# Staging weights in 1024-column buffers instead of 512-column ones in a one-core hybrid decoder step

## The chip, the core and the metric

The kernel runs on one NeuronCore of a Trainium2 chip as a single launch. The metric is the device time of one execution in microseconds. TensorE (PE in the profile, its weight loads PEld), VectorE (DVE), ScalarE (ACT), GpSimd (POOL) and SyncE (SP) each run their own instruction list in order and wait for each other through semaphores. SP starts the plain DMAs and POOL the indirect ones. The 16 DMA engines carry both.

## The reference

One layer of a decoder for 1024 prompt tokens and 32 sampled tokens, model width 1024, all in float32:

```
proj = x @ w_in                                # 1024 -> 9744 columns
o_a  = three dilated sliding-window softmax attentions, mixed by their log-sum-exp
o_b  = gated linear attention in chunks of 64, normalised, times silu(rb)
x    = layer_norm(a*x + (sigmoid(ga)*(o_a@w_branch_a) + sigmoid(gb)*(o_b@w_branch_b)) @ w_out)
q    = normalised (x @ w_peer_query)           # 8 heads
expert, gate = top 16 of 128 x 128 product keys per head     # 128 experts per token
act  = gelu(x . u_table[expert])
x    = layer_norm(a*x + sum(gate * act * v_table[expert]))
```

The caches of keys and values, moved on by the new tokens, and the states of the linear attention are outputs too.

## The kernel before

A float32 product is made of three TensorE passes (`mm3`, lines 184 to 187): every operand is split into a high part and a rest, both stored as fp32r, and high x high, rest x high and high x rest are added up. The split of a weight tile is two instructions: ACT copies the staged tile into the high part (`copy_act`, line 143) and DVE subtracts it to get the rest (line 158). Weights come through `load_w_` (line 170): one DMA of 128 x 512 floats into a staging buffer `wst` (three of them), a high part `wh` (four) and a rest `wl` (four). A staging buffer is free again when DVE has subtracted; a `wh` when TensorE has used it.

The program has these stretches. Prompt half b=0 (512 tokens) with the 32 sampled tokens, and then b=1 (512 tokens): projections (`dense_T` with 4 of 8 row blocks for one load, `rows_of` with one row block for one load), attention, linear attention, output projection, PEER queries and top-k. Then the PEER mixer, in two ways at once:

- `peer_gather` (line 1216), for half of the prompt tokens and the sampled ones: for each of 128 experts of a token tile, POOL gathers 128 rows of `u` (line 1233) or `v` (line 1254) into one of four `gr` buffers, and DVE makes one pass of 128 x 1024 over it (lines 1239 and 1272). That makes 1088 gathers, of which the last 32 of one tile are summed on TensorE.
- `peer_dense` (line 1330), for the other 512 tokens: all 16384 experts in 128 steps `e` of 128 experts. `hidden(e)` loads 128 columns of `uT` (two loads of 512) and makes 24 matmuls; `gelu` puts the result aside, seven steps ahead of its use. `values(e)` loads and splits 128 rows of `pv` (two loads of 512). `weights(e)` multiplies the gelu by the gate matrix `G` (line 1364), which is loaded for 8 steps at a time with two DMAs of 1 MB (line 1383, tensor `Gd`), and splits the product into two `tq` tiles. `out` makes 24 matmuls for each `e`. Eight steps are 384 matmuls of 512 columns; below they are called a block.

The ten `pg` pages hold the inputs of `hidden` (four), `G` and the split `v`. The order on each engine is not the order of the code: a scheduler places every instruction by priority and by its own estimate of time, and buffers that come free bound it. Gathers have the lowest priority and fill gaps. Weight loads get a higher priority than their place in the code. Buffers are named in rows by the helper's tag (`wst`, `wh`, `wl`, `pg`, `tq`, `gr`). The memory that the DMAs of POOL need for their descriptors lies in the same on-chip memory as the buffers, and its size is set where the program object is made, in `kernel` (line 1693).

Of the kernel before, what the change touches and what calls it, by code (L numbers as in the profile page):

```python
# [21 lines left out]
P = 128  # L22
# [59 lines left out]
def tile_hybrid_step(ctx, tc, I, O, dbg=None):  # L82
# [31 lines left out]
    def sb(shape, tag, bufs, dt=F32):  # L114
        return sp.tile(list(shape), dt, tag=tag, bufs=bufs, name=nm(tag))
# [42 lines left out]
        V.tensor_sub(lo, src, hi)  # L158

    copies = []  # L160
    due, hush = [0.0], [False]

    def load_w(src, shape):
        keep = tc.cur_priority
# [3 lines left out]
        return r  # L168

    def load_w_(src, shape):  # L170
        st = sb(shape, "wst", 3)
        ld = nc.sync.dma_start(st, src)
        due[0] += CRATE
        for _ in range(2):
            if copies and not hush[0] and due[0] >= 1:
                due[0] -= 1
                with tc.issue_after(ld.ins):
                    nc.sync.dma_start(*copies.pop(0))
        hi = sb(shape, "wh", 4, F32R)
        lo = sb(shape, "wl", 4, F32R)  # L180
        split_into(st, hi, lo)
        return hi, lo

    def mm3(out, lh, ll, rh, rl, first, last):
# [312 lines left out]
    def rows_of(toks, src, xs, cols=None, stag=0):  # L497

        outs = [(ps() if i < 4 else (pb if busy[0] else pc)())[:m] for i, m in toks]
        def products(p_, i, m, k, w):  # L500
            if i < 4 and cols:
                h, l = [cols(v, i) for v in xs(k, 0, T)]
            else:
                h, l = xs(k, i * P, i * P + m)
            mm3(p_, h, l, *w, k == 0, k == 7)


        for k in range(8):
            tick()
            if k <= 8 - stag:  # L510
                ws = []
            ws.append(load_w(src[:, k], [P, 512]))
            if k < 8 - stag:
                for p_, (i, m) in zip(outs, toks):
                    products(p_, i, m, k, ws[0])
        for p_, (i, m) in zip(outs, toks):
            for j in range(stag):
                products(p_, i, m, 8 - stag + j, ws[j])
        return outs


    def phase_a(b):

        mark(f"att{b}")
        dec = b == 0
        busy[0] = b == 1
        shapes = lambda d: (TW if d else T, [(0, 256), (256, TW)] if d else [(0, 512)], [(i, P) for i in range(4)] + [(4, NS)] * d)
        W, segs, toks = shapes(dec)
        row0 = lambda i: 2 * T if i == 4 else b * T + i * P
# [11 lines left out]
        def dense_T(src, nk, xs, width=P):  # L541

            out = [(ps(), c0, c1) for (c0, c1) in (segs0 if xs is x else segs)]
            for k0 in range(0, nk, 4):
                wh, wl = load_w(src[:, k0:k0 + 4], [P, 4, width])
                for k in range(k0, k0 + 4):
                    for (p_, c0, c1) in out:
                        h, l = xs(k, c0, c1)
                        mm3(p_[:width, :c1 - c0], wh[:, k - k0], wl[:, k - k0], h, l, k == 0, k == nk - 1)
            return out  # L550

        def proj_T(ci):
# [777 lines left out]
    def peer_dense(x1T, toks):  # L1330
# [4 lines left out]

        def hidden(e):
            p_ = ps()
            for k0 in (0, 4):
                wh, wl = load_w(I["uT"][e][:, k0:k0 + 4], [P, 4, P])
                for k in range(4):  # L1340
                    h, l = x1T(k0 + k, 0, T)
                    mm3(p_, wh[:, k], wl[:, k], h, l, k0 + k == 0, k0 + k == 7)
            return p_

        def values(e):
            v = page([P, 2, D], F32R)
            for hf in range(2):
                st = sb([P, 512], "wst", 3)
                c = slice(hf * 512, (hf + 1) * 512)
                nc.sync.dma_start(st, vrows[e][:, c])  # L1350
                split_into(st, v[:, 0, c], v[:, 1, c])
            return v

        def gelu(e):
# [351 lines left out]
```

## Time and profile before

| | |
|---|---|
| device time, median of 3 runs | 4181.1 us (4180.77 to 4182.56) |
| the profiled execution | 4168.93 us, of which the span of its instructions is 4167.2 us |
| PE busy | 3739.9 us (90%), 18338 matmuls |
| DVE busy | 3147.9 us (76%), 7279 instructions |
| ACT busy | 1444.7 us (35%), 2958 instructions |
| POOL busy | 1345.5 us (32%) |
| DMA | 1118.18 MB, mean 268 GB/s |
| PEER mixer's dense loop | first multiplication by G at 2598.6 us of the span, last block of G asked for at 4046.0 us |

Busy shares are means over stretches that differ, so the page's 40 slices and a table of stretches are read before any sum. A matmul of 512 columns is shown with some 0.4 us, but the next one starts 0.23 us later, since they overlap; what a stretch holds is read from counts of matmuls in a time. An idle stretch of an in-order engine is put down to the instruction that ended it.

### The profile page before, as it was taken

Reading aid. Unit: us, or ns where it says so; the run is one execution under the profiler, and the core shown is the slowest. Engines: PE = TensorE matmul, PEld = TensorE weight load, DVE = VectorE, ACT = ScalarE, POOL = GpSimd, SP = SyncE. Lnnn points to the kernel's source line nnn. Section 1 sums busy time; section 2 is a strip of 40 time slices with the busy share of each in tenths; the row PEclk is TensorE's granted clock in tenths of the full one; section 3 lists DMA queues with packets and bytes.
Section 4 is the critical chain, followed back from the end, with each engine's and each line's share of the span. In section 5 each row is a group of like instructions: output and inputs, shape, how many; then the busy total and the mean of one; then the engine's idle time right before and its main releaser. Section 6 shows DMA issues by size and latency. Waiting matters only on the chain.

```text
span 4167.2 us, 55732 instructions
## 1 busy us (share of the span) xinstructions
PE 3739.9 (90%) x18338; PEld 2890.6 (69%) x18338; DVE 3147.9 (76%) x7279; ACT 1444.7 (35%) x2958; POOL 1345.5 (32%) x1163
## 2 busy tenths in 40 slices
PE   8999999999897589999879866788999999999996
PEld 7888666665686478756757544677777777777775
DVE  2334433547999888788989998897888888888878
ACT  3334322324543354523225344332222233223323
POOL 0000000000245334354444322444444444444443
PEclk9999899999898689889889998999999999999997
DMA  8666465788688779778988756877998899999996
GB/s 276 199 215 201 164 201 184 262 272 277 200 310 299 226 260 327 255 243 304 317 300 283 222 199 241 274 249 269 312 311 310 309 318 311 318 318 320 312 320 248
DMA packets 455160, 1118.18 MB, mean 268 GB/s; under 512 B 48484, under 2 KB 133748, under 8 KB 444486
## 3 DMA queue, kind: packets, MB, share of 16 engines
q0 software_dynamic: 156672, 570.49, 39.8%
q1 hardware_dynamic: 298198, 544.13, 39.1%
q8 instruction: 144, 2.36, 0.2%
q14 instruction: 146, 1.20, 0.1%
HBM read 1043.94 MB, written 158.37 MB: 289 GB/s over the span
## 4 chain that ended last, share of the span: by engine, by line
PE 42%; DMA 20%; DVE 17%; issue 13%; POOL 5%; ACT 3%; SPq 0%; POOLq 0%; DVEq 0%; ACTq 0%
PE ps L185 9%; PE ps L186 9%; PE ps L187 9%; DMA gr<-pv,tkei 5%; DMA pg<-Gd 4%; POOL gr L1233 4%; DMA gr<-pu,tkei 3%; DVE gr L1239 3%; DMA wst<-pv 2%; DVE acc L1272 2%; DMA wst<-uT 2%; DVE wl L158 2%; PE pc L1312 2%; POOL gr L1254 2%; DVE tb L1309 1%
## 5 line engine op out<-in xcount | busy, mean ns | idle before, releaser
L1254 POOL DMA_INDIRECT gr<-pv,tkei x544 | 675.2, 1241 | 910.2 <-DVE acc L1272 567.3
L1233 POOL DMA_INDIRECT gr<-pu,tkei x544 | 651.1, 1197 | 951.3 <-DVE gr L1239 543.5
L185 PE MATMUL ps<-pg,wh 128*128 128x512 f32 (+3 forms) x2488 | 896.7, 362 | 65.7 <-ACT wh L143 43.5
L186 PE MATMUL ps<-pg,wl 128*128 128x512 f32 (+3 forms) x2488 | 896.0, 360 | 8.8 <-DVE wl L158 8.6
L187 PE MATMUL ps<-pg,wh 128*128 128x512 f32 (+3 forms) x2488 | 892.5, 360 | 0.0
L143 ACT ACTIVATE wh<-wst 128x512 fp32r<-128x512 f32 x740 | 462.2, 628 | 1148.7 <-DMA wst<-uT 347.7
L158 DVE TENSOR_TENSOR wl<-wst,wh 128x512 fp32r<-128x512 f32 x740 | 502.5, 683 | 346.1 <-ACT wh L143 317.2
L1239 DVE SCALAR_TENSOR_TENSOR gr<-gr,x1g 128x1024 f32<-128x1024 f32 x544 | 660.4, 1220 | 121.5 <-DMA gr<-pu,tkei 119.8
L1272 DVE SCALAR_TENSOR_TENSOR acc<-gr,act,acc 128x1024 f32<-128x1024 f32 x512 | 654.9, 1279 | 70.8 <-DMA gr<-pv,tkei 67.4
L185 PEld LDWEIGHTS ps<-pg,wh 128*128 128x128 f32 (+1 forms) x2488 | 472.2, 190 | 162.7 <-ACT wh L143 49.6
L186 PEld LDWEIGHTS ps<-pg,wl 128*128 128x128 f32 (+1 forms) x2488 | 472.9, 190 | 91.1 <-DVE wl L158 13.3
L187 PEld LDWEIGHTS ps<-pg,wh 128*128 128x128 f32 (+1 forms) x2488 | 472.5, 190 | 77.1 <-issue 10.7
L185 PE MATMUL ps<-wh,pg 128*128 128x512 f32 x832 | 342.2, 418 | 33.2 <-ACT wh L143 20.3
L186 PE MATMUL ps<-wh,pg 128*128 128x512 f32 x832 | 341.6, 411 | 3.7 <-DVE pg L158 3.7
L187 PE MATMUL ps<-wl,pg 128*128 128x512 f32 x832 | 323.5, 415 | 4.0 <-DVE wl L158 3.6
L143 ACT ACTIVATE pg<-wst 128x512 fp32r<-128x512 f32 x256 | 160.0, 630 | 448.0 <-DMA wst<-pv 428.8
L185 PEld LDWEIGHTS ps<-wh,pg 128*128 128x128 f32 x832 | 177.6, 214 | 90.3 <-ACT wh L143 26.7
L1046 POOL MEMSET tq<- 128x512 f32 x6 | 3.2, 526 | 661.7 <-issue 287.2
L187 PEld LDWEIGHTS ps<-wl,pg 128*128 128x128 f32 x832 | 174.9, 213 | 51.8 <-issue 10.8
L185 PE MATMUL ps<-tq,pg 128*128 128x512 f32 x512 | 203.4, 400 | 7.9 <-ACT t L1356 7.8
L186 PEld LDWEIGHTS ps<-wh,pg 128*128 128x128 f32 x832 | 177.4, 213 | 44.1 <-issue 10.5
L186 PE MATMUL ps<-tq,pg 128*128 128x512 f32 x512 | 202.4, 395 | 0.0
(421 smaller groups left out, 5728.0 us busy)
## 6 DMA issues: line engine op xcount, KB each, us to landing
o_old<-cache SPq DMA_DIRECT2D x256, 256.0 KB
wst<-uT SPq DMA_DIRECT2D x256, 256.0 KB
wst<-pv SPq DMA_DIRECT2D x256, 256.0 KB
wst<-wT SPq DMA_DIRECT2D x192, 256.0 KB
Gd<-pg SPq DMA_DIRECT2D x32, 1024.0 KB
pg<-Gd SPq DMA_DIRECT2D x32, 1024.0 KB
wst<-wN SPq DMA_DIRECT2D x112, 256.0 KB
wst<-wq SPq DMA_DIRECT2D x96, 256.0 KB
```

The lines of the kernel that those rows point to most:

```text
L143: nc.scalar.activation(out, in_, AF.Copy, scale=scale)
L158: V.tensor_sub(lo, src, hi)
L185: nc.tensor.matmul(out, lh, rh, start=first, stop=False)
L186: nc.tensor.matmul(out, ll, rh, start=False, stop=False)
L187: nc.tensor.matmul(out, lh, rl, start=False, stop=last)
L1046: nc.gpsimd.memset(qf, 0.0)
L1233: nc.gpsimd.indirect_dma_start(out=u, out_offset=None, in_=I["pu"], in_offset=bass.IndirectOffsetOnAxis(ap=ei[:, j:j + 1], axis=0))
L1239: V.scalar_tensor_tensor(u, u, 1.0, x1, ALU.mult, ALU.mult, accum_out=act[:, j:j + 1])
L1254: nc.gpsimd.indirect_dma_start(out=u, out_offset=None, in_=I["pv"], in_offset=bass.IndirectOffsetOnAxis(ap=ei[:, j:j + 1], axis=0))
L1272: V.scalar_tensor_tensor(acc, u, act[:, j:j + 1], acc, ALU.mult, ALU.add, accum_out=None if j < n - 1 or decode else sums[:, 0, 0:1])
L1309: last.append(V.tensor_scalar(og[:, k], consts["rows"], eT[:, 1, n:n + 1], eT[:, 2, n:n + 1], ALU.is_equal, ALU.mult))
L1312: nc.tensor.matmul(p_[:, k], o1[:, k], og[:, k], start=True, stop=True)
```

## The change

Staging, high and rest buffers become 1024 columns wide: three `wst`, two `wh` and three `wl`, 32 KB of a partition where it was 22 KB. The memory that the program object reserves for the descriptors of POOL's DMAs is set to 4 KB of a partition. For b=0 (`fine`), a buffer is filled by two DMAs and split in two halves, so those loads and splits keep 512 columns (`wa`, with four row blocks, gets halves of 256). For b=1 and the dense loop, a load is one DMA of 512 KB, and its split is one ACT and one DVE instruction of 1024 columns. `dense_T` and `hidden` take all row blocks in one load, `rows_of` two, `values` one load of 1024.

```diff
 def load_w_(src, shape):
-    st = sb(shape, "wst", 3)
-    ld = nc.sync.dma_start(st, src)
-    due[0] += CRATE
-    for _ in range(2):
...
-    hi = sb(shape, "wh", 4, F32R)
-    lo = sb(shape, "wl", 4, F32R)
-    split_into(st, hi, lo)
+    raw = sb(shape, "wst", 3)
+    hi = sb(shape, "wh", 2, F32R)
+    lo = sb(shape, "wl", 3, F32R)
+    half = shape[1] // 2
+    parts = [slice(0, half), slice(half, None)] if fine[0] else [slice(None)]
+    for c in parts:
+        ld = nc.sync.dma_start(raw[:, c], src[:, c])
+        due[0] += CRATE * 2 / len(parts)
+        for _ in range(4 // len(parts)):
...
+    for c in parts:
+        split_into(raw[:, c], hi[:, c], lo[:, c])
     return hi, lo
 # rows_of
+    if k % 2 == 0:
+        wh, wl = load_w(src[:, k:k + 2], [P, 2, 512])
-    ws.append(load_w(src[:, k], [P, 512]))
+    ws.append((wh[:, k % 2], wl[:, k % 2]))
 # phase_a
+    fine[0] = b == 0
 # dense_T
-    for k0 in range(0, nk, 4):
-        wh, wl = load_w(src[:, k0:k0 + 4], [P, 4, width])
+    wh, wl = load_w(src, [P, nk, width])
 # peer_dense.hidden
-    for k0 in (0, 4):
-        wh, wl = load_w(I["uT"][e][:, k0:k0 + 4], [P, 4, P])
+    wh, wl = load_w(I["uT"][e], [P, 8, P])
 # peer_dense.values
-    for hf in range(2):
-        st = sb([P, 512], "wst", 3)
...
+    st = sb([P, D], "wst", 3)
+    nc.sync.dma_start(st, vrows[e])
+    split_into(st, v[:, 0], v[:, 1])
 # kernel
-    nc = bacc.Bacc("TRN2", target_bir_lowering=False, num_devices=1)
+    nc = bacc.Bacc("TRN2", target_bir_lowering=False, num_devices=1, dynamic_dma_scratch_size=4096)
```

The scheduler also orders everything anew. Three places, all around the same load of G (the eighth pair of 16), follow; line numbers after the change are 4 to 7 higher there.

On SP, before: the two loads of G (`pg<-Gd`) among loads of 512 columns of `uT` and `pv`.

```order
L172 DMA wst_29085<-uT 128x512
L1350 DMA wst_29123<-pv 128x512
L1350 DMA wst_29127<-pv 128x512
L172 DMA wst_29139<-uT 128x512
L1383 DMA pg_29210<-Gd 128x16x128
L1383 DMA pg_29211<-Gd 128x16x128
L172 DMA wst_29157<-uT 128x512
L1350 DMA wst_29215<-pv 128x512
```

On SP, now:

```order
L1354 DMA wst_27464<-pv 128x1024
L178 DMA wst_27476<-uT 128x1024
L1354 DMA wst_27526<-pv 128x1024
L178 DMA wst_27538<-uT 128x1024
L1387 DMA pg_27603<-Gd 128x16x128
L1354 DMA wst_27608<-pv 128x1024
L1387 DMA pg_27604<-Gd 128x16x128
L178 DMA wst_27620<-uT 128x1024
```

Before, half a chunk of `uT` stands behind G; now the whole chunk of the step, and the one of the step before, stand ahead of it.

On DVE, before: from the subtraction that frees the staging buffer for the last `uT` load ahead of G (`wl_29088`) to the first multiplication by G.

```order
L158 TENSOR_TENSOR wl_29088<-wst_29085,wh_29087 128x512
L1272 SCALAR_TENSOR_TENSOR acc_23965<-gr_24134,act_23533,acc_23965 128x1024
L158 TENSOR_TENSOR pg_29122<-wst_29123,pg_29122 128x512
L1272 SCALAR_TENSOR_TENSOR acc_23965<-gr_24137,act_23533,acc_23965 128x1024
L158 TENSOR_TENSOR pg_29122<-wst_29127,pg_29122 128x512
L1272 SCALAR_TENSOR_TENSOR acc_23965<-gr_24140,act_23533,acc_23965 128x1024
L1399 TENSOR_TENSOR tb_22360<-tb_22360,ps_29034 128x512
L1272 SCALAR_TENSOR_TENSOR acc_23965<-gr_24143,act_23533,acc_23965 128x1024
L158 TENSOR_TENSOR tq_29134<-tb_28585,tq_29133 128x512
L1399 TENSOR_TENSOR tb_22361<-tb_22361,ps_29042 128x512
L158 TENSOR_TENSOR wl_29142<-wst_29139,wh_29141 128x512
L1364 TENSOR_TENSOR t_5989_28657<-t_5989_28657,pg_29210 128x256
```

On DVE, now (the subtraction that frees the staging buffer, `wl_27400`, stands four rows above the first one here, with two passes over gathered rows and one L1403 between):

```order
L158 TENSOR_TENSOR pg_27525<-wst_27526,pg_27525 128x1024
L1279 SCALAR_TENSOR_TENSOR acc_22838<-gr_22974,act_22406,acc_22838 128x1024
L158 TENSOR_TENSOR tq_27393<-tb_26910,tq_27392 128x512
L1403 TENSOR_TENSOR tb_21356<-tb_21356,ps_27315 128x512
L158 TENSOR_TENSOR tq_27471<-t_5047_26972,tq_27470 128x512
L1279 SCALAR_TENSOR_TENSOR acc_22838<-gr_22977,act_22406,acc_22838 128x1024
L1279 SCALAR_TENSOR_TENSOR acc_22838<-gr_22980,act_22406,acc_22838 128x1024
L1279 SCALAR_TENSOR_TENSOR acc_22838<-gr_22983,act_22406,acc_22838 128x1024
L1368 TENSOR_TENSOR t_5069_27116<-t_5069_27116,pg_27603 128x256
L1368 TENSOR_TENSOR tb_27194<-tb_27194,pg_27603 128x256
L1368 TENSOR_TENSOR t_5089_27256<-t_5089_27256,pg_27603 128x256
L158 TENSOR_TENSOR wl_27478<-wst_27476,wh_27477 128x1024
```

The rest of one `uT` chunk (`wl_27478`) now stands behind the first multiplications by G, and six passes over gathered rows stand between the freed buffer and G where four stood.

On ACT, before: the copy that needs both halves of G (`tq_29225`), and what is queued behind it.

```order
L143 ACTIVATE pg_29122<-wst_29123 128x512
L143 ACTIVATE pg_29122<-wst_29127 128x512
L143 ACTIVATE tq_29133<-tb_28585 128x512
L143 ACTIVATE wh_29141<-wst_29139 128x512
L143 ACTIVATE tq_29225<-t_5989_28657 128x512
L143 ACTIVATE wh_29159<-wst_29157 128x512
L1356 ACTIVATE tb_29065<-ps_29066 128x512
L143 ACTIVATE pg_29214<-wst_29215 128x512
```

On ACT, now (the copy is `tq_27614`):

```order
L143 ACTIVATE wh_27477<-wst_27476 128x1024
L1360 ACTIVATE tb_27334<-ps_27335 128x512
L143 ACTIVATE wh_27539<-wst_27538 128x1024
L1360 ACTIVATE t_5109_27396<-ps_27397 128x512
L143 ACTIVATE tq_27532<-tb_27054 128x512
L143 ACTIVATE pg_27607<-wst_27608 128x1024
L143 ACTIVATE tq_27614<-t_5069_27116 128x512
L143 ACTIVATE pg_27669<-wst_27670 128x1024
L143 ACTIVATE wh_27621<-wst_27620 128x1024
```

Before, the second half of the `uT` chunk in work (`wh_29159`) stood behind that copy; now two whole chunks stand ahead of it.

## Rows read from the trace of the kernel before

**Rows 1.** windows: busy us of each engine (x instructions), granted clock, DMA share, GB/s.

```profile
0.00:1000.00 1000.00, 969.36 (x5795) 724.81 (x5796) 415.21 (x995) 317.10 (x755) 17.57 (x68) 0.97 0.67 222
1000.00:2600.00 1600.00, 1344.34 (x6560) 1024.17 (x6559) 1428.18 (x4074) 652.46 (x1389) 626.22 (x525) 0.89 0.79 266
2990.00:4046.00 1056.00, 1003.14 (x4233) 803.87 (x4232) 875.80 (x1314) 314.47 (x537) 483.52 (x407) 0.97 0.90 313
4046.00:4167.00 121.00, 82.63 (x349) 66.62 (x347) 95.12 (x150) 37.11 (x69) 38.67 (x32) 0.82 0.74 261
```

**Rows 2.** waits of PE from 2990 to 4046 us: total us, times, longest.

```profile
PE ps L185 <- ACT wh L143: 39.6, 11, 5.3
PE ps L186 <- DVE wl L158: 5.2, 5, 2.0
PE ps L185 <- DVE tb L1399: 3.7, 7, 1.0
PE ps L185 <- ACT t L1356: 3.6, 6, 1.0
```

**Rows 3.** timeline of SP: start us, us, instruction.

```profile
3281.26 0.33 SPq L172 DMA_DIRECT2D wst<-uT  x1
3281.64 5.45 SPq L1383 DMA_DIRECT2D pg<-Gd  x2
3287.19 8.77 SPq L172 DMA_DIRECT2D wst<-uT  x1
```

**Rows 4.** timeline of DVE, ACT, PE just after; brackets: idle before, and what ended it.

```profile
3295.63 0.43 DVE L1364 TENSOR_TENSOR t<-t,pg 128x256 f32<-128x256 f32 x1 [4.45 <-DMA pg<-Gd]
...
3299.67 0.42 DVE L1364 TENSOR_TENSOR t<-t,pg 128x256 f32<-128x256 f32 x1 [2.27 <-DMA pg<-Gd]
...
3300.19 0.63 ACT L143 ACTIVATE tq<-t 128x512 fp32r<-128x512 f32 x1 [13.49 <-DVE t L1364]
...
3301.39 0.80 PE L185 MATMUL ps<-pg,wh 128*128 128x512 f32 x1 [3.37 <-ACT wh L143]
...
3302.41 0.63 PE L187 MATMUL pb<-tq,pg 128*128 128x512 f32 x1
3302.84 0.63 PE L185 MATMUL pc<-tq,pg 128*128 128x512 f32 x1
...
3308.08 0.39 PE L187 MATMUL ps<-pg,wh 128*128 128x512 f32 x1
```

**Rows 5.** windows of one block: the load of G, and the time after it.

```profile
3281.00:3308.00 27.00, 23.19 (x88) 18.11 (x88) 18.86 (x30) 5.61 (x10) 8.20 (x8) 0.87 0.83 279
3308.00:3380.30 72.30, 70.34 (x304) 56.46 (x303) 61.98 (x74) 22.27 (x38) 37.92 (x31) 1.00 0.92 319
```

**Rows 6.** groups by line and shape, whole span: busy us, mean ns, idle before.

```profile
L158 DVE TENSOR_TENSOR wl<-wst,wh 128x512 fp32r<-128x512 f32 x736 | 501.7, 686 | 344.2 <-ACT wh L143 315.3 <-PE ps L186 9.0 <-DMA o_old<-cache 4.1
```

**Rows 7.** one line: a DVE pass over 128 x 1024; ns min/median/max.

```profile
L966 DVE TENSOR_TENSOR acc<-acc,gr x5: 1207/1220/1226, 1867.7 to 4161.1; 128x1024 f32<-128x1024 f32 x4, 32x1024 f32<-32x1024 f32 x1
```

**Rows 8.** waits of DVE from 2990 to 4046 us.

```profile
DVE t L1364 <- DMA pg<-Gd: 65.7, 21, 7.3
DVE gr L1239 <- DMA gr<-pu,tkei: 32.1, 37, 3.0
DVE acc L1272 <- DMA gr<-pv,tkei: 30.3, 31, 2.4
```

**Rows 9.** waits of PE in the first 1000 us.

```profile
PE ps L185 <- ACT wh L143: 12.9, 3, 11.8
```

**Rows 10.** DMA queues from 2990 to 4046 us: packets, MB, share of 16 engines.

```profile
q0 software_dynamic: 58338, 212.42, 56.2%
q1 hardware_dynamic: 96715, 117.54, 34.0%
```

**Rows 11.** the gathers into gr: ns min/median/max, first and last start.

```profile
L1254 POOL DMA_INDIRECT gr<-pv,tkei x544: 935/1145/4178, 1402.6 to 4132.0; - x182
```

More of the change, by code (lines that the diff above doesn't have):

```diff
@@ L160, in tile_hybrid_step @@
     copies = []
-    due, hush = [0.0], [False]
+    due, hush, fine = [0.0], [False], [True]
     def load_w(src, shape):
@@ L170, in load_w_ @@
     def load_w_(src, shape):
-        st = sb(shape, "wst", 3)
-        ld = nc.sync.dma_start(st, src)
-        due[0] += CRATE
-        for _ in range(2):
[L175 to L178, printed above, removed]
-        hi = sb(shape, "wh", 4, F32R)
-        lo = sb(shape, "wl", 4, F32R)
-        split_into(st, hi, lo)
+        raw = sb(shape, "wst", 3)
[7 more added lines that the diff above has]
+            for _ in range(4 // len(parts)):
+                if copies and not hush[0] and due[0] >= 1:
+                    due[0] -= 1
+                    with tc.issue_after(ld.ins):
+                        nc.sync.dma_start(*copies.pop(0))
+        for c in parts:
+            split_into(raw[:, c], hi[:, c], lo[:, c])
         return hi, lo
@@ L543, in dense_T @@
             out = [(ps(), c0, c1) for (c0, c1) in (segs0 if xs is x else segs)]
-            for k0 in range(0, nk, 4):
-                wh, wl = load_w(src[:, k0:k0 + 4], [P, 4, width])
[L546 to L549, printed above, removed]
+            wh, wl = load_w(src, [P, nk, width])
+            for k in range(nk):
+                for (p_, c0, c1) in out:
+                    h, l = xs(k, c0, c1)
+                    mm3(p_[:width, :c1 - c0], wh[:, k], wl[:, k], h, l, k == 0, k == nk - 1)
             return out
@@ L1337, in hidden @@
             p_ = ps()
-            for k0 in (0, 4):
-                wh, wl = load_w(I["uT"][e][:, k0:k0 + 4], [P, 4, P])
-                for k in range(4):
-                    h, l = x1T(k0 + k, 0, T)
-                    mm3(p_, wh[:, k], wl[:, k], h, l, k0 + k == 0, k0 + k == 7)
+            wh, wl = load_w(I["uT"][e], [P, 8, P])
+            for k in range(8):
+                h, l = x1T(k, 0, T)
+                mm3(p_, wh[:, k], wl[:, k], h, l, k == 0, k == 7)
             return p_
@@ L1346, in values @@
             v = page([P, 2, D], F32R)
-            for hf in range(2):
-                st = sb([P, 512], "wst", 3)
-                c = slice(hf * 512, (hf + 1) * 512)
-                nc.sync.dma_start(st, vrows[e][:, c])
-                split_into(st, v[:, 0, c], v[:, 1, c])
+            st = sb([P, D], "wst", 3)
+            nc.sync.dma_start(st, vrows[e])
+            split_into(st, v[:, 0], v[:, 1])
             return v
```

## The prediction, made before the changed kernel had run

> **What bounds the kernel now.** I read the table of stretches first. Up to 1000 us PE is busy for 969 of 1000 us; from 1000 to 2600 us DVE leads with 1428 of 1600 (89%), PE has 1344 at a granted clock of 0.89; from 2990 to 4046 us, eleven equal blocks of the dense loop, PE has 1003 of 1056 and DVE 876 [rows 1]. So the loop is PE's, with 52 us idle. PE's waits there name the cause: four rows hold 39.6 + 5.2 + 3.7 + 3.6 = 52.1 us, and the first is eleven stalls, one a block, for an ACT copy of a weight [rows 2]. The copy is only where it shows. In SP's timeline the two G DMAs are asked for at 3281.64, right behind a `uT` load [rows 3]; DVE reaches its multiplications by G at 3295.63 and 3299.67 after idling 4.45 and 2.27 us for them, ACT's `tq` copy behind it has waited 13.49 us, and the `wh` copy behind that one lets PE run dry for 3.37 us [rows 4]. [...]
>
> One block is 384 matmuls in 96.0 us (1056/11). Away from G it runs 304 in 72.3 us, 0.238 each, so an undisturbed block takes 91.3 us. The stretch with G takes 27 us for 88 matmuls that would take 20.9: 6.1 us lost at one G load [rows 5]. Sixteen pairs of G are loaded, fifteen of them behind the start of the loop.
>
> **The G load, where most of the forecast lies.** SP asks in order, so G is asked for when the `uT` load ahead of it gets its staging buffer, that is when DVE has made an earlier rest. Counted in the orders: before, that rest is `wl_29088`, and the first matmul that needs anything queued behind G (`wh_29159`, on ACT) comes 28 matmuls after the first use of `wl_29088`. Now the rest is `wl_27400`, and the first matmul that needs anything behind G (`wl_27478`, on DVE) comes 72 after its first use. The ask is 44 matmuls earlier against PE's need: 44 x 0.238 = 10.5 us. Three things eat into it. DVE has six gather passes instead of four between the freed buffer and G, with the splits 12.7 us of work by the rows' durations instead of 9.0 (4 us). Up to 512 KB more stand ahead of G in the queues; at 313 GB/s [rows 1] that is 1.7 us. And the lead that DVE and ACT can have over PE is smaller: two `wh` of 1024 come free whole, where four of 512 came free one by one. [...] I take it that the third spoils part of the blocks and the stop falls from 6.1 to 2.5 us, 60% gone. Ends: nothing gained, or all 6.1. 15 x 3.6 = **-54 us**.
>
> **Merged splits.** By the program there are 364 pairs of splits that become one: 256 in the dense loop, 108 in b=1. A split of 512 costs DVE 0.686 us [rows 6]; the nearest row of 1024 columns with two tensors in is L966, 1.220 us [rows 7]. A pair saves 2 x 0.686 - 1.220 = 0.15 us. In the loop the 39 us hide behind PE; they only shorten DVE's queue. In b=1, DVE-bound at 89%, 108 x 0.15 = 16 us, of which I put half on the path: **-8 us** (ends 0 and -16). On ACT the copy of 1024 is not in the trace; between one and two of the 0.63 us copies [rows 4] it adds nothing in an engine busy 314 of 1056 us [rows 1], but the first half of a weight is ready up to 0.6 us later, which only a PE that has run dry would notice.
>
> **The tail.** After the loop only gathers are left. Counted in DVE's order, at step 120 of 128 the changed order has done 1012 of them where before had 1025, and it has 6 left behind the last `out` instead of 2. A gather takes 1056/407 = 2.59 us in the loop [rows 1]. Between 4 x 2.6 = 10 and 13 x 2.6 = 34 us, I take **+15 us**, near the count at the end, because the DMA share in the last stretch falls to 0.74 [rows 1] and leaves room.
>
> **b=0 and the fewer buffers.** In b=0 loads and splits stay at 512, so nothing merges; but two wide `wh` are freed whole, so the copies run at most some 28 matmuls ahead of PE in the projections instead of 41 (counted). PE waited for `wh` there 12.9 us in 1000 [rows 9]. From 0 to doubling that, I take **+2 us**; the same loss of lead in b=1 could cost as much again, and is in the range.
>
> **Sum.** -54 - 8 + 15 + 2 = -45 us. The profiled execution is 4168.9 us (span 4167.2), so 4124 by its own clock; the median of the runs lies 12.2 us above it, which gives 4136.
>
> **Rivals.**
>
> Longer packets make the gathers late: slower. The weight DMAs share the 16 engines with the gathers, 34.0% and 56.2% of their time in the loop [rows 10]. By time for a MB (0.562 x 16 x 1056/212.42 = 44.7 us for q0 with pieces of 4 KB, 0.340 x 16 x 1056/117.54 = 48.9 us for q1, mostly 2 KB) a piece takes 0.18 and 0.10 us. A gather has 58338/407 = 143 packets, 9 on each engine. If at each of them a piece of the other queue goes first, the doubled pieces cost it 9 x 0.08 = 0.7 us. Four `gr` buffers are turned over in 4 x 2.59 = 10.4 us; a gather 0.7 us longer makes each cost 0.7/4 more where DVE already waits for it. That is 562 gathers from 2590 to 4046 us x 0.17 = up to 98 us; it decides from where gathers, not PE, set the block, and DVE waits for them only 62.4 us in 1056 today [rows 8], so I take 70%: +69, and the sum of -45 against it leaves +24, 4205. Against it: by the same two rows 4 KB pieces need 8% less engine time for each MB. [...]
>
> The gathers' ring takes over: no change. DVE's 875.8 busy, 65.7 waiting for G and 62.4 for gathers make 1004 of 1056 us [rows 1, 8]; the DMA share is 0.90 [rows 1]. If the idle time for G only turns into waits for gathers, a block shrinks by 1 us: -15, -8, +15, +2 = -6: 4175.
>
> All of the stop goes, and in b=1 all 16 us of the splits show: 15 x 6.1 = 92 + 16, less 10 for the tail: 4083.
>
> The 4 KB descriptor memory holds gathers back. A gather's instruction takes POOL 1.145 us in the median, 4.178 at most [rows 11], so some already wait. Four `gr` buffers let only four gathers be in flight, before and now, 4 x 144 = 576 packets. If a smaller memory made POOL wait 1.2 us more for each, a gather (0.3 us a turn) x 562 = +169 with the G gain lost, less 8, with 17 of tail and b=0: about 4360; I take 4300, a third of it hidden by the buffers that are ahead. Nothing in the rows says how many packets a KB holds. [...]
>
> **Numbers.** My forecast 0.48 (its own range 4100 to 4165), all gone 0.13, no change 0.15, longer packets 0.17, descriptor memory 0.07. A measurement of this kernel tells about 0.2%, 8.4 us, from no change. The no-change case splits 0.04, 0.09, 0.02 over the three; so faster 0.48 + 0.13 + 0.04 = 0.65, same 0.09, slower 0.17 + 0.07 + 0.02 = 0.26. From 4075 to 4205 the range leaves out some 0.04 below and 0.15 above.
>
> **What would show it.** Right: blocks of about 92.5 us between G asks instead of 96.0; PE idle after a G load mostly gone and the granted clock near 1.00 in all of the loop; DVE's waits for G well below 65.7 us; splits of 1024 at 1.2 us; POOL's gather still 1.1 us. The tail shows as more time between the last `out` and the end. Wrong: PE stalls still eleven times at G; DVE waits for gathers well above 62.4 us (packets, or the ring); gather instructions on POOL much above 1.145 us (memory); waits for `wh` in the first 2600 us far above 12.9 us (too few buffers), the term I have bounded least well.

## The result: 0.7% slower, and the profile after

The changed kernel takes 4213.5 us in the median of seven runs (4197.9 to 4235.9), where before takes 4181.7 us on the same chips: ratio 1.007, 95% interval 1.0048 to 1.0092. The prediction had 4136 us and a range that ended at 4205. The profiled execution takes 4205.38 us, its span 4203.6 us.

Both kernels start 18338 matmuls, so the time at which the k-th one starts shows where they part (us after the same matmul of before, from the traces; the repeat in the last column has the order of before and differs by scatter alone, up to 16 us):

| k | before starts at | after | e1_scratch4 (order of before) |
|---|---|---|---|
| 1000 | 177.3 | +17 | +1 |
| 9500 | 1878.4 | +14 | -13 |
| 11500 | 2335.0 | +46 | -12 |
| 12500 | 2641.2 | +35 | -12 |
| 15500 | 3430.2 | +16 | -16 |
| 17500 | 3927.4 | +23 | -9 |
| 18337 | 4141.4 | +30 | -7 |

So 17 us go at the very start and some 30 in b=1 between matmuls 9500 and 11500. In the first half of the dense loop 19 come back, and 14 go again in its second half and at the end; these two are of the size of the scatter. The stretches, with the loop from the fifth to the last load of G (columns as in [rows 1]):

```profile
0.00:1000.00 1000.00, 953.73 (x5689) 722.46 (x5689) 390.48 (x925) 306.20 (x754) 18.88 (x68) 0.96 0.66 221
1000.00:2600.00 1600.00, 1327.69 (x6538) 1006.82 (x6535) 1409.10 (x3938) 618.15 (x1257) 669.75 (x515) 0.89 0.77 261
2997.00:4056.00 1059.00, 999.02 (x4227) 805.03 (x4226) 857.28 (x1146) 279.81 (x361) 552.13 (x404) 0.98 0.90 311
4056.00:4204.00 148.00, 100.34 (x427) 80.56 (x425) 116.13 (x158) 38.40 (x63) 57.41 (x46) 0.84 0.74 260
```

Eleven blocks of the loop take 1059.5 us, 96.3 each, where [rows 1] had 96.0 and the repeat, e1_scratch4, has 97.1: no gain. DVE is busy 18 us less, POOL 69 us more. PE's and then DVE's waits in the same stretch:

```profile
PE ps L190 <- DVE tb L1403: 54.1, 26, 5.3
PE ps L190 <- ACT t L1360: 5.8, 3, 2.6
```

```profile
DVE gr L1246 <- DMA gr<-pu,tkei: 72.0, 49, 4.4
DVE t L1368 <- DMA pg<-Gd: 65.4, 17, 8.3
DVE acc L1279 <- DMA gr<-pv,tkei: 56.1, 48, 4.0
```

The stalls for `wh` on ACT, 39.6 us of the 52.1 in [rows 2], are gone, and DVE's additions to `tb` (L1403), 3.7 us before, now hold PE for 54.1. DVE still waits 65 us for G, as in [rows 8], and for gathers 128 us instead of 62. The eighth load shows the new chain; SP, then DVE, then PE:

```profile
3279.61 0.33 SPq L178 DMA_DIRECT2D wst<-uT  x1
3279.99 0.43 SPq L1387 DMA_DIRECT2D pg<-Gd  x1
3286.16 1.69 SPq L1354 DMA_DIRECT2D wst<-pv  x1
3287.90 0.43 SPq L1387 DMA_DIRECT2D pg<-Gd  x1
```

```profile
3302.57 0.43 DVE L1368 TENSOR_TENSOR t<-t,pg 128x256 f32<-128x256 f32 x1 [6.64 <-DMA pg<-Gd]
...
3309.31 0.68 DVE L1403 TENSOR_TENSOR tb<-tb,ps 128x512 f32<-128x512 f32 x1
```

```profile
3310.05 0.50 PE L190 MATMUL ps<-pg,wh 128*128 128x512 f32 x1 [2.42 <-DVE tb L1403]
```

The second half of G is asked for 8 us behind the first, with a `pv` load of 512 KB in between. DVE stands idle 6.64 us for it; the addition that frees PE's accumulator is queued behind, and PE waits for that.

The time for a gather's POOL instruction, over the whole span (compare [rows 11]); the share over 1.5 us is 389 of 1088 where it was 193, by count in the traces:

```profile
L1261 POOL DMA_INDIRECT gr<-pv,tkei x544 | 744.7, 1369 | 855.6 <-DVE acc L1279 466.9
L1240 POOL DMA_INDIRECT gr<-pu,tkei x544 | 721.4, 1326 | 894.5 <-DVE gr L1246 497.6
```

Before, their means were 1241 and 1197 ns. Two lines of time show why, POOL and then DVE of the changed kernel:

```profile
3617.73 0.94 POOL L1240 DMA_INDIRECT gr<-pu,tkei  x1 [0.30 <-issue]
3619.32 1.68 POOL L1240 DMA_INDIRECT gr<-pu,tkei  x1 [0.65 <-DVE gr L1246]
...
3626.00 0.94 POOL L1240 DMA_INDIRECT gr<-pu,tkei  x1 [0.30 <-issue]
```

```profile
3617.82 1.23 DVE L1246 SCALAR_TENSOR_TENSOR gr<-gr,x1g 128x1024 f32<-128x1024 f32 x1 [1.19 <-DMA gr<-pu,tkei]
...
3618.97 1.22 DVE L158 TENSOR_TENSOR wl<-wst,wh 128x1024 fp32r<-128x1024 f32 x1
...
3626.00 1.25 DVE L158 TENSOR_TENSOR pg<-wst,pg 128x1024 fp32r<-128x1024 f32 x1
```

A gather that starts with DVE idle or together with a DVE instruction takes 0.94 us. The one that starts 0.35 us into a 1.22 us subtraction ends 0.81 us behind that subtraction's end. Of the gathers behind 2600 us, 117 start well inside a subtraction of 1024 columns (0.1 us or more after its start, 0.13 us or more ahead of its end) and take 1.68 us in the median; before, 249 started so inside a subtraction of 512 columns and took 1.15. In both kernels they end 0.81 us behind the subtraction. It goes with what DVE reads: the 40 gathers that start so inside L1403, one of whose two inputs is PE's accumulator, take 0.94 us, as this one does, and the pass that starts inside that gather is no longer than others (rows of DVE, POOL and DVE):

```profile
3621.91 0.69 DVE L1403 TENSOR_TENSOR tb<-tb,ps 128x512 f32<-128x512 f32 x1
3622.27 0.94 POOL L1240 DMA_INDIRECT gr<-pu,tkei  x1 [1.27 <-DVE gr L1246]
3622.51 1.22 DVE L1246 SCALAR_TENSOR_TENSOR gr<-gr,x1g 128x1024 f32<-128x1024 f32 x1
```

A gather is often released by DVE's pass over its buffer, so it meets whatever DVE does next, which is now the long subtraction.

At the start of the program, 140 to 160 us, before and then after:

```profile
140.00:160.00 20.00, 19.53 (x156) 17.29 (x156) 8.87 (x25) 8.06 (x23) 0.00 (x0) 1.00 0.51 175
```

```profile
140.00:160.00 20.00, 16.00 (x81) 11.42 (x78) 7.06 (x30) 6.46 (x24) 0.00 (x0) 0.50 0.28 84
```

Attention's small matmuls of the first group (L361, L387, L393) stand alone on PE there: 83 of them in a row in the trace (the expectations below give the row as 24 long), where before has at most 34 between matmuls of the projections. An idle time of 2.74 us opens up just ahead of them, others of 2.04 and 0.47 us among them; from 140.1 us on the granted clock is 0.50 for 23.9 us, and 81 matmuls run in these 20 us where before has 156.

### The profile page after: what moved, and what is told of

It reads as the page before. It is cut to its first block, busy times and chain, and to the rows that moved or that the text cites. A ratio compares the mean times of both kernels' runs of the same rounds, so it can differ in the third digit from the quotient of the medians.

```text
span 4203.6 us, 53661 instructions
## 1 busy us (share of the span) xinstructions
PE 3724.6 (89%) x18338; PEld 2892.4 (69%) x18338; DVE 3116.6 (74%) x6922; ACT 1369.8 (33%) x2601; POOL 1486.6 (35%) x1163
## 4 chain that ended last, share of the span: by engine, by line
PE 28%; DMA 20%; issue 20%; DVE 15%; POOL 10%; ACT 3%; SPq 0%; POOLq 0%; DVEq 0%; ACTq 0%
DMA gr<-pv,tkei 10%; POOL gr L1240 7%; DMA gr<-pu,tkei 6%; PE ps L190 6%; PE ps L191 6%; PE ps L192 6%; POOL gr L1261 3%; DVE gr L1246 3%; DVE acc L1279 3%; DMA pg<-Gd 3%; PE pc L1319 1%; DVE wl L158 1%; PE pb L361 1%; ACT pg L143 1%; PE pb L1135 1%
## 5 line engine op out<-in xcount | busy, mean ns | idle before, releaser
L1261 POOL DMA_INDIRECT gr<-pv,tkei x544 | 744.7, 1369 | 855.6 <-DVE acc L1279 466.9
L1240 POOL DMA_INDIRECT gr<-pu,tkei x544 | 721.4, 1326 | 894.5 <-DVE gr L1246 497.6
L1246 DVE SCALAR_TENSOR_TENSOR gr<-gr,x1g 128x1024 f32<-128x1024 f32 x544 | 658.7, 1225 | 181.8 <-DMA gr<-pu,tkei 180.8
L143 ACT ACTIVATE wh<-wst 128x512 fp32r<-128x512 f32 (+3 forms) x511 | 405.0, 816 | 894.1 <-PE ps L192 519.9
L158 DVE TENSOR_TENSOR wl<-wst,wh 128x512 fp32r<-128x512 f32 (+3 forms) x511 | 464.8, 924 | 226.9 <-ACT wh L143 221.3
L143 ACT ACTIVATE pg<-wst 128x1024 fp32r<-128x1024 f32 x128 | 135.3, 1057 | 447.6 <-DMA wst<-pv 337.7
```

Source lines behind the costliest of these rows:

```text
L143: nc.scalar.activation(out, in_, AF.Copy, scale=scale)
L1240: nc.gpsimd.indirect_dma_start(out=u, out_offset=None, in_=I["pu"], in_offset=bass.IndirectOffsetOnAxis(ap=ei[:, j:j + 1], axis=0))
L1246: V.scalar_tensor_tensor(u, u, 1.0, x1, ALU.mult, ALU.mult, accum_out=act[:, j:j + 1])
L1261: nc.gpsimd.indirect_dma_start(out=u, out_offset=None, in_=I["pv"], in_offset=bass.IndirectOffsetOnAxis(ap=ei[:, j:j + 1], axis=0))
```

## The experiments

Eight kernels (labels e) tell the parts of the change apart, then four (f) and two (g) what holds the loop. Each was timed in five rounds beside before, whose median lay between 4177.9 and 4181.6 us there, and the ratio is to those runs; "gather" is the mean of POOL's instruction, "waits" DVE's for gathers, both from 2990 to 4050 us; a block runs from one load of G to the next, PE idle is for eleven of them.

| run | median us | ratio (95%) | block us | waits us | PE idle us | gather ns |
|---|---|---|---|---|---|---|
| before | 4181.7 | 1 | 96.0 | 62 | 53 | 1192 |
| after | 4213.5 | 1.007 (1.0048 to 1.0092) | 96.3 | 128 | 60 | 1375 |
| e1_scratch4 | 4179.7 | 1.0011 (0.9995 to 1.0027) | 97.1 | 67 | 60 | 1188 |
| e2_sub_halves | 4244.6 | 1.0153 (1.0125 to 1.018) | 97.1 | 114 | 72 | 1201 |
| e3_load_halves | 4208.6 | 1.0084 (1.0056 to 1.0112) | 96.7 | 121 | 57 | 1355 |
| e4_all_halves | 4213.1 | 1.0078 (1.0052 to 1.0104) | 96.0 | 76 | 56 | 1252 |
| e5_gr6 | 4328.5 | 1.0358 (1.0329 to 1.0388) | 107.0 | 34 | 171 | 1330 |
| e6_same_mem512 | 4162.6 | 0.9959 (0.9943 to 0.9975) | 95.7 | 84 | 51 | 1212 |
| e7_366 | 4209.8 | 1.0075 (1.0049 to 1.0101) | 97.3 | 58 | 73 | 1222 |
| e8_wide_wst2_gr5 | 4170.5 | 0.9975 (0.9957 to 0.9993) | 98.3 | 66 | 65 | 1353 |
| f1_446_gr5 | 4059.2 | 0.9713 (0.9682 to 0.9743) | 90.4 | 45 | 12 | 1289 |
| f2_544_gr6 | 4045.9 | 0.9683 (0.9652 to 0.9714) | 88.3 | 10 | 0 | 1327 |
| f3_wide_wst2_wh3 | 4172.0 | 0.9996 (0.9971 to 1.002) | 96.2 | 118 | 62 | 1319 |
| f4_one_g | 4148.8 | 0.9925 (0.99 to 0.995) | - | 50 | - | 1226 |
| g1_wide_gr5 | 4155.3 | 0.9951 (0.9933 to 0.9968) | 89.0 | 42 | 6 | 1383 |
| g2_wide_242 | 4220.8 | 1.0098 (1.0079 to 1.0118) | 96.0 | 130 | 61 | 1358 |

In the diffs `...` marks lines left out: the same change in `values` and at other places that use the buffer, and in e5, e6, e7, f1 and f2 the 4 KB of descriptor memory as in e1.

**e1_scratch4.** Before, with only the descriptor memory changed.

```diff
-    nc = bacc.Bacc("TRN2", target_bir_lowering=False, num_devices=1)
+    nc = bacc.Bacc("TRN2", target_bir_lowering=False, num_devices=1, dynamic_dma_scratch_size=4096)
```

> The kernel before with the descriptor memory of 4 KB and nothing else changed; the order of all instructions is the same as before. Theory A (a gather's instruction on POOL cannot go on while a DVE instruction runs, and the 1024-column subtractions last 1.2 us instead of 0.7): same as before, 4175 to 4190 us, gather instruction 1.22 us in the mean, DVE waiting 187 us for gathers in all. Theory B (4 KB pieces of the weight loads delay the gathers in the DMA engines): the same as A here. Theory C (the smaller descriptor memory holds the gathers up): gather instructions 1.35 us in the mean, waits for gathers near 300 us, 4195 to 4215 us.

As A and B had it: the time is that of before, the gather 1188 ns. Theory C, the fourth rival's mechanism, is out.

**e2_sub_halves** and **e3_load_halves.** The first cuts only DVE's subtractions in two, the second only the loads.

```diff
# e2
         for c in parts:
-            split_into(raw[:, c], hi[:, c], lo[:, c])
+            copy_act(hi[:, c], raw[:, c])
+        for c in (slice(0, half), slice(half, None)):
+            V.tensor_sub(lo[:, c], raw[:, c], hi[:, c])
...
# e3
-        for c in parts:
+        for c in (slice(0, half), slice(half, None)):
             ld = nc.sync.dma_start(raw[:, c], src[:, c])
...
```

> The changed kernel, but every subtraction of 1024 columns on DVE is two of 512; loads, copies on ACT and buffers stay wide. Theory A: the gather's mean on POOL falls from 1.35 to about 1.24 us, DVE's waits for gathers from 2990 to 4050 us fall from 128 to some 80 to 95 us, and the time by 10 to 25 us (4190 to 4205), since 364 x 0.15 = 55 us of DVE work come back. Theory B: gather instruction and waits may move, the round trip behind POOL's instruction (6.1 us) does not, and the time stays at 4213 or rises by the added DVE work to 4235. Theory C: gather instruction stays at 1.35 us.

> The changed kernel, but every load of 1024 columns is two DMAs of 512 columns (2 KB pieces); splits stay 1024 wide. Theory A: gather instruction stays at 1.35 us, waits for gathers near 128 us from 2990 to 4050 us, time 4205 to 4220. Theory B: waits for gathers fall to 62 to 80 us there, the time from POOL's end to DVE's start from 6.1 back to 5.9 us or less, time 4180 to 4195. Theory C: as A.

Each takes back one part of a gather's longer round trip. POOL's groups from 2990 to 4050 us, of e2 and of e3:

```profile
L1242 POOL DMA_INDIRECT gr<-pu,tkei x206 | 241.9, 1174 | 310.4 <-DVE gr L1248 265.5 <-issue 21.3 <-ACT gr L963 8.9
L1263 POOL DMA_INDIRECT gr<-pv,tkei x190 | 233.6, 1229 | 275.5 <-DVE acc L1281 234.2 <-issue 15.5 <-DMA gr<-pv,tkei 11.5
```

```profile
L1261 POOL DMA_INDIRECT gr<-pv,tkei x207 | 289.2, 1397 | 256.7 <-DVE acc L1279 210.6 <-DMA gr<-pv,tkei 16.8 <-issue 16.1
L1240 POOL DMA_INDIRECT gr<-pu,tkei x196 | 256.7, 1310 | 259.9 <-DVE gr L1246 221.6 <-issue 26.5 <-DVE acc L1279 3.6
```

With subtractions of 512, POOL's instruction is back at 1201 ns; the time from its end to DVE's pass, for the gathers of `u` that DVE waited for, stays long (6.31 us, 6.14 after, 5.94 before). With loads of 512 it is the other way round: 5.77 us, and 1355 ns on POOL. So A and B are both at work, 0.3 and 0.2 us of a round trip of 7.22 us before and 7.71 after. But neither alone brings DVE's waits for gathers back: 114 us in e2 where theory A expected 80 to 95, and 121 in e3, which is what theory A expected of it. Nor did either give the time that its own theory expected: e3 is as slow as after, and e2 is 31 us slower. DVE is busy 27 us more in e2 than in after (3143.9 and 3116.6 us), which can be most of that; no run shows it alone.

**e4_all_halves.** Wide buffers, everything in halves.

```diff
-    fine[0] = b == 0
+    fine[0] = True
...
```

> The changed kernel's buffers of 1024 columns, but all loads and all splits in halves of 512, as b=0 has them. A and B alike: gather instruction 1.24 us, waits for gathers from 2990 to 4050 us 60 to 80 us. What is left against the kernel before is then the buffers' number and the new order: start-up 16 us and what b=1 loses for that reason, so 4180 to 4200; if the loop keeps the G gain of 22 us, 4165 to 4180. Theory C: gather instruction 1.35 us, 4200 or more.

Gather and waits came back as expected, the time did not: 19 us late at matmul 1000, 57 at 11500. What is lost ahead of the loop does not come from the size of loads and splits. And with the waits for gathers back at 76 us the blocks still take 96.0: DVE waits 88 us for G instead of 65, and 22 for ACT's copies instead of 5.

**e5_gr6.** Six gather buffers for four in the memory that is freed; weights as before.

```diff
-    u = sb([P, D], "gr", 4)
+    u = sb([P, D], "gr", 6)
...
```

> The kernel before with the 4 KB descriptor memory and, in the memory this frees, six gather buffers instead of four; weights stay at 512 columns. Ring theory (a gather's round trip of 7.2 to 7.7 us against the DVE work between a buffer's pass and its next one sets DVE's waits): with six buffers the work between is half as long again, so the waits for gathers fall from 187 us in all to under 40; in b=1, where DVE sets the time, some 30 to 50 us are gained there, in the loop little, since the stop at G stays: 4125 to 4160. Rival (the waits come from the DMA engines being full, share 0.90): gathers only start earlier and land later, the waits stay above 120 us, 4170 to 4185.

The waits fell as expected and the time rose by 150 us. The planner fills DVE's gaps with gathers, and with three staging buffers it now finds room for 7.3 a step instead of 4.5 (counted in DVE's order: 1011 of them are ahead of step 80, where before has 839). PE then waits for the copies and splits of weights (first two rows, 2990 to 3900 us); from 4050 us on no gather is left and DVE, busy 120 of the last 279 us, mostly idles (the window of the last row reaches past the end):

```profile
PE ps L185 <- ACT wh L143: 86.3, 16, 13.9
PE ps L186 <- DVE wl L158: 64.9, 42, 3.5
```

```profile
4050.00:4400.00 350.00, 259.48 (x1147) 212.31 (x1145) 119.99 (x215) 89.31 (x159) 0.00 (x0) 0.98 0.29 89
```

**e6_same_mem512** and **e7_366.** Buffers of 512 columns in the freed memory: six staging, four high, six low, and three, six, six.

```diff
# e6
-    st = sb(shape, "wst", 3)
-    lo = sb(shape, "wl", 4, F32R)
+    st = sb(shape, "wst", 6)
+    lo = sb(shape, "wl", 6, F32R)
...
# e7
-    hi = sb(shape, "wh", 4, F32R)
-    lo = sb(shape, "wl", 4, F32R)
+    hi = sb(shape, "wh", 6, F32R)
+    lo = sb(shape, "wl", 6, F32R)
...
```

> The kernel before with 4 KB of descriptor memory and the changed kernel's buffer memory cut in buffers of 512 columns: six for staging, four high, six low. Depth theory (six staged pieces let the planner run the projections' weights ahead, so that the attention of the first group stands alone on PE for 24 matmuls at half clock): 15 to 19 us late by matmul 1000, as the changed kernel is. Width theory (buffers of 1024 that come free only whole): no delay there, 0 to 3 us. In b=1 and the loop the gather instruction is back at 1.22 us and its waits at 36 + 38 and 62 us; the G stop should be smaller with deeper staging. Depth theory 4175 to 4195, width theory 4150 to 4175.

> The kernel before with 4 KB of descriptor memory and six high and six low buffers of 512 columns, but three for staging. Depth theory (staging alone makes the gap at the start): matmul 1000 at the time of before, within 2 us; G is still asked for late because staging is as shallow, so the G stop stays and the time is that of before, 4165 to 4182. Rival (more high and low buffers let ACT and DVE run ahead and take the stop at G away): PE's waits for high parts from 2990 to 4046 us fall from 39.6 to under 15 us, 4130 to 4160.

e6 loses the start as after does (16 us at matmul 1000), without a wide buffer, as the depth theory had it, though its time, 4163, is below that theory's range. Its stretch from 140 to 160 us has the same few matmuls at a clock of 0.56:

```profile
140.00:160.00 20.00, 16.02 (x74) 11.63 (x75) 8.12 (x34) 6.97 (x24) 0.00 (x0) 0.56 0.16 47
```

e7, with staging no deeper, was late by 8 us where 2 were expected, so depth is not all of it; its time, 4210, lies 28 us above the depth theory's range. In b=1, from matmul 9800 to 10200, e6 and e7 lose nothing (-2 and -1 us), the wide kernels (after, e2, e3, e4) 15 to 23. With more high and low buffers alone, PE's stall moved from `wh` to L1399 (48.2 us) and did not shrink; the rival of e7 is out.

**e8_wide_wst2_gr5.** After, with two staging buffers and five gather buffers.

```diff
-    raw = sb(shape, "wst", 3)
+    raw = sb(shape, "wst", 2)
-    u = sb([P, D], "gr", 4)
+    u = sb([P, D], "gr", 5)
...
```

> The changed kernel with two staging buffers of 1024 columns instead of three and, in their place, five gather buffers instead of four. Ring theory: DVE's waits for gathers fall from 307 us in all to 80 to 120, b=1 and the late loop come back to or below the times of before; depth theory: half of the start-up loss goes (the row of attention matmuls alone is 14 long instead of 24). Together 4150 to 4185. If the width of the buffers itself costs b=1 its time, the delay of 20 to 30 us from matmul 9500 to 11500 stays and the time is 4195 or more.

The start is back (+1 us at matmul 1000), b=1 still loses 28 us, the waits halve. A block carries 39.5 gathers instead of 36.5 and is 2 us longer, and 7 gathers are left at 4050 us instead of 47.

**f1_446_gr5** and **f2_544_gr6.** Buffers of 512 columns; deeper staging and more gather buffers together.

```diff
# f1
-    st = sb(shape, "wst", 3)
-    lo = sb(shape, "wl", 4, F32R)
-    u = sb([P, D], "gr", 4)
+    st = sb(shape, "wst", 4)
+    lo = sb(shape, "wl", 6, F32R)
+    u = sb([P, D], "gr", 5)
...
# f2
-    st = sb(shape, "wst", 3)
-    u = sb([P, D], "gr", 4)
+    st = sb(shape, "wst", 5)
+    u = sb([P, D], "gr", 6)
...
```

> The kernel before with 4 KB of descriptor memory and buffers of 512 columns (four staging, four high, six low), and five gather buffers. Ring theory (DVE is as full as PE in the loop, and what its waits for gathers give back is gained): waits for gathers from 2990 to 4050 us fall from 62 to 30 to 45 us, 15 to 35 us gained over the whole program; depth theory: matmul 1000 late by 3 to 8 us (the attention row alone is 14 matmuls long); width theory: no loss from matmul 9800 to 10100. Together 4140 to 4165. Rival (more gathers in flight slow the loop, as with six buffers and shallow staging, +150 us): by the planner's order the last multiplication by G has 1039 gathers before it where the kernel before has 1035, so not here; if it is so all the same, 4200 or more.

> The kernel before with 4 KB of descriptor memory, five staging buffers of 512 columns instead of three and six gather buffers instead of four. Ring theory: waits for gathers from 2990 to 4050 us under 30 us instead of 62, in b=1 half of 74; 25 to 45 us gained, less the start-up (17 attention matmuls alone: 5 to 12 us): 4140 to 4165. Rival (starved loop as in the run with six gather buffers and three staging buffers): blocks of over 105 us and 4280 or more; the planner's order speaks against it, with 1041 gathers before the last multiplication by G, where that run had all 1056 by three quarters of the loop.

The direction was right and the size far off: 122 and 136 us gained, at least three times what was expected, and f2 is the fastest kernel of the study. At matmul 1000 f1 is 5 us late, as expected, and f2 17, where 5 to 12 were. DVE's and PE's waits of f2 from 2990 to 3900 us:

```profile
DVE t L1364 <- DMA pg<-Gd: 51.6, 18, 5.3
DVE tb L1399 <- PE ps L187: 20.3, 16, 2.5
DVE wl L158 <- ACT wh L143: 8.6, 13, 1.3
DVE acc L1272 <- DMA gr<-pv,tkei: 7.2, 4, 2.6
```

```profile
PE ps L185 <- DVE tb L1399: 0.2, 1, 0.2
```

DVE waits for G almost as long as ever, and PE never notices: DVE now runs ahead of PE (it waits for PE's results, second row) and spends that lead at G. A block is 88.3 us, less than the floor of 91.3 taken from [rows 5].

**f3_wide_wst2_wh3.** After, with two staging and three high buffers.

```diff
-    raw = sb(shape, "wst", 3)
-    hi = sb(shape, "wh", 2, F32R)
+    raw = sb(shape, "wst", 2)
+    hi = sb(shape, "wh", 3, F32R)
...
```

> The changed kernel with two staging buffers and three high ones of 1024 columns, instead of three and two. Theory 'two high buffers are too few' (ACT's copies wait for whole buffers): the loss from matmul 9800 to 10100 in b=1 falls from 17 us to 5 or less. Theory 'width' (the weights come in lumps of 1024 however many buffers): 14 us or more stay. By the depth theory matmul 1000 is late by 5 us or less instead of 17. So 4175 to 4190 by the first, 4190 to 4205 by the second.

The time is that of before, below both ranges: the start costs 6 us instead of 17. From matmul 9800 to 10100, the stretch that was named, 13.9 us are lost where after loses 19, which is as good as the 14 or more of the width theory; to 10200 it is 10.5.

**f4_one_g.** Before, without fifteen of the sixteen pairs of G loads.

```diff
-            if e % 8 == 0:
+            if e == 0:
```

> The kernel before with G loaded once: the other fifteen pairs of loads are left out, and all steps use the gates of the first eight. It prices the stop at G. By the prediction's term (6.1 us of PE time at each of fifteen loads) 85 to 95 us are gained, blocks of 91 to 92 us, about 4090. By the theory that DVE and the ring of gather buffers are as full as PE: the gathers take the time, 40 or more of them a block instead of 37, blocks of 94 us or more, waits for gathers above 62 us, and 30 to 60 us gained, mostly behind the loop: 4120 to 4150.

Every step then uses the gates of the first eight. With those loads gone, matmuls 12500 to 17500 take 1284 us; with them 1286. More gathers run in the loop (431 from 2990 to 4050 us instead of 408), and DVE is busy 31 us more there. The rest went into other waits of DVE: for ACT's copies 97 us instead of 46. From matmul 17500 to the end the trace gains 14 us, with fewer gathers left; the traced executions differ by 10 us in all, so where the rest of the 33 in the medians was gained is not shown. PE still waits for DVE and ACT (2990 to 3900 us):

```profile
DVE pg L158 <- ACT pg L143: 57.3, 37, 3.8
PE ps L185 <- ACT t L1356: 26.5, 18, 3.7
PE ps L185 <- DVE tb L1399: 23.9, 21, 2.9
```

**g1_wide_gr5.** The changed kernel with a fifth gather buffer, and 2 KB of descriptor memory to make room for it.

```diff
-    u = sb([P, D], "gr", 4)
+    u = sb([P, D], "gr", 5)
...
-    nc = bacc.Bacc("TRN2", target_bir_lowering=False, num_devices=1, dynamic_dma_scratch_size=4096)
+    nc = bacc.Bacc("TRN2", target_bir_lowering=False, num_devices=1, dynamic_dma_scratch_size=2048)
```

> The changed kernel with five gather buffers instead of four (2 KB of descriptor memory make the room), all else as it is. Ring theory (the loop of the changed kernel stands where it stood because the four gather buffers turn over too slowly for the freed DVE time): waits for gathers from 2990 to 4050 us fall from 128 to 40 to 70 us, blocks from 96.3 to 90 to 92 us, PE's idle time in eleven blocks from 60 to under 25 us; the start-up loss of 17 us and b=1's stay, so 4130 to 4155. Rival (what freed the loop in the two runs with five and six gather buffers is the staging in pieces of 512, not the ring): blocks of 95 us or more, 4195 to 4215.

One more gather buffer, and the changed kernel's loop goes from 96.3 to 89.0 us a block, PE's idle time from 60 to 6 us, the time from 4213 to 4155. DVE's wait for G is still there (2990 to 3900 us), PE's has gone:

```profile
DVE t L1368 <- DMA pg<-Gd: 62.4, 16, 7.7
```

```profile
PE ps L190 <- DVE tb L1403: 6.3, 6, 2.1
```

Staging in pieces of 512 is not needed for it. Ahead of the loop this kernel is 66 us behind before (matmul 11500; after is 46), so the wide buffers' loss there stays.

Read beside the others, g1 shows that the gather buffers are half of it. With more of them and shallow staging the loop is no faster: 107.0 us a block in e5 (three pieces of 512) and 98.3 in e8, which is g1 with one wide staging buffer fewer and 4 KB of descriptor memory. With deep staging and four gather buffers it is not either: 95.7 in e6, 96.3 in after. All three kernels with both (f1, f2, g1) are at 88 to 90. Every one of these kernels also has an order of its own from the planner (e8 has more gathers in a block), and no run holds the order fixed.

**g2_wide_242.** After, with two staging, four high and two low buffers.

```diff
-    raw = sb(shape, "wst", 3)
-    hi = sb(shape, "wh", 2, F32R)
-    lo = sb(shape, "wl", 3, F32R)
+    raw = sb(shape, "wst", 2)
+    hi = sb(shape, "wh", 4, F32R)
+    lo = sb(shape, "wl", 2, F32R)
...
```

> The changed kernel with two staging, four high and two low buffers of 1024 columns (three, two and three before). Theory 'high buffers' (ACT's copies stand behind whole buffers that PE still reads): the loss from matmul 9800 to 10200, 16 us with two high buffers and 10 with three, is 5 us or less with four; time 4160 to 4180. Theory 'width' (lumps of 1024, however many): 10 us or more stay, 4175 to 4200; two low buffers instead of three could then cost more, up to 4215.

From matmul 9800 to 10200 21.5 us are lost, so more high buffers do not mend it (this kernel also has one low buffer fewer, and its time, 4221, is above every range that was given). That it is the width fits all eight wide kernels (10 to 27 us there) against e6 and e7 (none); f1 and f2, also of 512 columns, lose 8 and 10 in the same place, so more is at work, and it stays open.

## Why the prediction was wrong

**The G stop (-54 us): this step failed.** Its first half held: G is asked for earlier against PE, 65 to 108 matmuls from the fifth pair on instead of the 44 counted (the eighth pair at matmul 14827 instead of 14916). But DVE's multiplication moved up with the load (matmul 14879 instead of 14974), about 13 us behind the ask as before, and DVE's wait stayed at 65 us, where a sign of being right was a wait well below 65.7. That 2.5 of the 6.1 us would be left of the stop was the author's estimate, and no run shows it: PE's idle time in eleven blocks was 60 us after, where before had 53. And "the first matmul that needs anything behind G" was looked for among weights only: PE needs its accumulators too, and L1403, which frees them, is queued on DVE behind G. The deeper fault is the premise that the loop was PE's with a stop at G. f4 takes the stop away and the loop does not move: more gathers and longer waits for ACT's copies fill DVE's time. What decides whether PE sees a wait of DVE is DVE's lead over PE, as f2 and g1 show: DVE waits for G almost as long as ever (51.6 and 62.4 us from 2990 to 3900 us), and PE hardly for DVE (0.2 and 6.3 us).

**The gathers' ring.** The no-change rival said it: a block shrinks by 1 us or not at all. Its sum (875.8 + 65.7 + 62.4 of 1056) stood in the rows and was given 0.15. The sum by itself proves little, since the busy time and all the waits of an engine always make up the stretch (the missing 52 are mostly DVE's waits for ACT's copies, 45.9); what counts is that one wait gave way to another. What the rival missed is that the round trip gets longer. For each of 402 gather passes before and 399 after I took from the trace DVE's time between that pass and the one four later: it spreads alike (median 7.9 and 8.1 us). Adding up what is missing to 7.2 us gives 59 us for before (measured 61); missing to 7.7 us, 131 for after (measured 126). By this sum half a microsecond on a ring of four costs 66 us, about what the merged splits and the waits for ACT had set free (18 us of DVE's busy time, and its waits for ACT's copies in the same stretch, 45.9 us before and 5.2 after). That this is what kept the block at 96 us is argued and not shown: in e4 the waits for gathers fall back to 76 us, and the block stays. What is shown is that a fifth gather buffer beside three wide staging buffers frees it (g1).

**The longer-packets rival** had the right place and a share of the size: 0.2 us of a gather instead of 0.7. The other 0.3 us, POOL held up by longer DVE instructions, was no rival at all.

**Merged splits (-8 us in b=1).** This term was mis-sized. The durations are as read, 1225 ns for 1024 columns against 2 x 686, but DVE starts its next instruction 0.08 us before one is shown to end: without idle time between, starts are 0.603 us apart behind 512 columns and 1.136 behind 1024 (medians). A pair saves 0.07 us and not 0.15, and DVE's busy time in all fell by 31 us (3147.9 to 3116.6), not 55. From 1000 to 2600 us DVE is busy 19 us less and waits 44 us more for gathers (118 instead of 74 from 1000 to 2500 us), so nothing of it is seen to reach the end.

**b=0 and the fewer buffers (+2 us)** was the term called least well bounded, and it was +14 to +17 at the start and about +30 in b=1, outside its own bounds. It looked at the lead of copies, and there it was right: PE's waits for `wh` in the first 1000 us went from 12.9 to 15.1. The price at the start came from the planner's new order and the lower clock that went with it (0.50 for 23.9 us, after; 0.56 from 140 to 160 us, e6); where that of b=1 comes from stays open.

**The tail (+15 us).** From the ask for the last G to the end it was 121 us and is 147, but that ask now comes at an earlier matmul (17915 instead of 17990); after loses 7 us from matmul 17500 to the last one and 6 behind it, 13 in all. The term held, about as well as the scatter lets one say.

**The descriptor memory** was rightly held harmless: with 4 KB e1 takes 4179.7 us, and its gather 1188 ns on POOL where before has 1192.

## What to carry to other kernels

A stall is a price only if the engine behind it has no lead to spend: before pricing a stop, ask which of that engine's other waits would take its place, and treat a ring of buffers whose round trip is near its turn as an engine of its own. Time taken off such an engine can come back as waits unless everything that feeds it has slack: here more gather buffers alone and deeper staging alone left the loop where it was or made it slower, and both together freed it. The freed memory was worth 32 us lost as wider weight buffers and 136 us gained as gather and staging buffers. What a merged instruction saves is read from the distance between starts, not from durations that overlap (here 0.07 us a pair, where the durations give 0.15). More buffers also change what a greedy planner does first, so a change of buffers is read from the planner's new order at every stage, not only at the one that it is meant for.

## What the runs showed of the hardware

A gather's instruction on POOL takes 0.94 us in the median when it starts with no DVE instruction under way (170 of them before, 168 after). From 2600 us on, one that starts well inside a DVE subtraction, which reads two buffers, ends 0.81 us behind that subtraction's end: it takes 1.68 us in the median inside subtractions of 1024 columns (117, after) and 1.15 us inside ones of 512 (249, before). Inside L1403, which reads one buffer and an accumulator, it takes 0.94 us (40, after). The other way round no hold shows: subtractions of 1024 columns last 1.22 us in the median whether they start inside a gather (151) or not (213). The gather's instruction as a whole is held; what in it waits no run tells apart.
